# Seven products for eight in the second MLP product of a two-layer decoder trunk

## The chip, the core and the metric

One NeuronCore of a Trainium2 chip runs the whole program in one launch. The metric is the device time of one execution in microseconds (us), the median of several runs. Five engines work beside each other, each through its own queue in order: PE (TensorE, matmuls), DVE (VectorE), ACT (ScalarE), POOL (GpSimd) and SP (SyncE, which issues the loads).

## The reference, cut to what matters

The program is two layers of a decoder on 256 tokens of width 1024, in float32. Each layer has a mixer and an MLP; only the MLP is touched by the change.

```python
def sqrelu_mlp(hn, w1, w2):
    return jnp.square(jax.nn.relu(hn @ w1)) @ w2          # w1: 1024 x 4096, w2: 4096 x 1024

for i in range(DEPTH):                                    # DEPTH = 2
    ...                                                   # x = x + mixer(rms_norm(x))
    x = x + sqrelu_mlp(rms_norm(x, norm_mlp[i]), mlp_w1[i], mlp_w2[i])
return rms_norm(x, norm_final)
```

## The kernel before, in words

**Three matmuls for one product.** Every operand of a matmul is held as a rounded high part and a low part that is the rest, and a product is three matmuls into one PSUM bank: high by high, high by low, low by high (`mm3`, L532 to L536). So each weight block that is loaded must first be split: ACT copies it into the high part (L475), DVE subtracts that from the raw block and writes the low part (L478). Both of DVE's inputs lie in SBUF.

**Pieces.** All weights come as a stream of 128 x 1024 pieces in the order in which they are used (`_blocks`). `loads` (L452) brings each into one of five raw buffers by an SP transfer, as buffers come free; `splits` (L461) takes a pair of high and low buffers from the pool `parts`, issues the two split steps and gives the raw buffer back. A piece's pair goes back to `parts` when its last matmul is done. `parts` has six pairs, and two more while the MLP runs (`spare_m`).

**The MLP** (`mlp`, L1357). The 4096 hidden columns are worked in 16 pairs of 128-column tiles (`NI` = 16). For a pair i, the up-projection `cols_T` makes two 128 x 256 tiles in one bank: 2 columns of 8 steps of 3 matmuls of 256 columns, 48 in all. `square` (L1362) makes the squared relu: ACT takes the relu (L1368) and the square's high part (L1370), POOL multiplies the relu by itself in float32 (L1371), DVE subtracts (L1373). The down-projection (`down`, L1419) multiplies the pair by two pieces of the second weight: for a pair, 2 tiles (a) x 2 halves of the tokens (t) x 2 halves of the output columns (n), so 8 products of 3 matmuls of 512 columns, 24 in all, into four banks, one for each (t, n). The loop at L1427 interleaves the up-projection of pair i + 1 with the down-projection of pair i. The last three pairs (`TAIL` = 3) are kept for the end (the tail, L1444 to L1456), where one bank after the other is finished by 18 matmuls and added to x (L1310).

**The order of the work** is written by a planner when the kernel is built. Each step has a duration that the planner assumes (`t_act`, `t_dve`, a number for POOL), an urgency and events that it waits for; the planner runs these through a model and emits each engine's instructions in the order in which they came up. On the chip each engine keeps that order and waits by semaphores.

Of the kernel before, what the change touches and what calls it, by code (L numbers as in the profile page):

```python
# [73 lines left out]
def _blocks(ins):  # L74
# [6 lines left out]
    def n(w, k0, k1, cols):  # L81
        return np.asarray(w[k0 * 128:k1 * 128, cols]).reshape(k1 - k0, 128, -1).transpose(1, 0, 2)
# [7 lines left out]
    def span(a, b):  # L90
        return np.arange(a, b)
# [38 lines left out]
    mlp(0)  # L130
# [12 lines left out]
    return cut  # L143


def _lay_out(ins):
    f = {k: np.asarray(ins[k]) for k in ins}
    blocks = _blocks(ins)
# [167 lines left out]
class Slots:  # L316
# [4 lines left out]

    def get(self, n=1):
        ev = Event()
        self.waiting.append((ev, n))
        self.serve()
        return ev
# [23 lines left out]
    def serve(self):  # L350
        while self.waiting and len(self.items) >= self.waiting[0][1]:
            ev, n = self.waiting.pop(0)
            got, self.items = self.items[:n], self.items[n:]
            self.plan.fire(ev, "slot", got if n > 1 else got[0])
# [9 lines left out]
def trunk_kernel(ctx: ExitStack, tc: tile.TileContext, x, w, prm_d, gs, cst_d, eye, out, widths):  # L364
    nc = tc.nc

    hot = ctx.enter_context(tc.tile_pool(name="hot", bufs=1))
# [61 lines left out]
    class Piece:  # L429
        count, current, uses = 0, 0, 0  # L430

        def __init__(self):
            self.p, self.ready, self.slots = Piece.count, Event(), parts
            Piece.count += 1

        def use(self):
            Piece.current = max(Piece.current, self.p)
            Piece.uses += 1

        def release(self, ev):  # L440
# [11 lines left out]
    def loads():  # L452
        for p, n in enumerate(widths):
# [5 lines left out]
            plan.when([ev], None, lambda p=p, raw=got.value: plan.fire(loaded[p], SP, raw))  # L459

    def splits():  # L461
        for p, n in enumerate(widths):
            pc = pieces[p]
            yield loaded[p]
            got = pc.slots.get()
            yield got
# [414 lines left out]
    KK = [G1[:, 2560:3072].rearrange("p (a t) -> p a t", a=2), acts.tile([128, 2, S], F32R, name="KK")]  # L881
    KL = acts.tile([128, 2, 2, S], F32R, name="KL")
    KZ = acts.tile([128, 2, 2, S], F32R, name="KZ")
    gates = acts.tile([128, 2, 3, 2, 4], F32, name="gates")
# [16 lines left out]
    def first_norms():  # L901
        def keep_on():

            z = tbuf.items[1][0]
            yield zero_e
            while Piece.uses < KEEP:
                yield pe(0.23, lambda: nc.tensor.matmul(banks[1].t, z[:, :128], z, start=True, stop=True), u=9)  # L907

# [447 lines left out]

    def mlp(src, x_ready, nxt):  # L1357

        NI = FF // 256
        hs = [Event() for _ in range(NI)]  # L1360

        def square(i, b, deps, slots):  # L1362
            got = pbuf.get(2)
            tgot = tbuf.get()
            yield [got, tgot]
            r, sq = got.value
            hh, hl = tgot.value
            e = act(t_act(512), lambda: nc.scalar.activation(r, b.t, AF.Relu), got, *deps)  # L1368
            slots.put(b, [e])
            f = act(t_act(512, False), lambda: nc.scalar.activation(hh, r, AF.Square), e, tgot)  # L1370
            g = pool(1.225, lambda: nc.gpsimd.tensor_tensor(sq, r, r, OP.mult), e)  # L1371
            pbuf.put(r, [f, g])
            h = dve(t_dve(512), lambda: nc.vector.tensor_tensor(hl, sq, hh.bitcast(F32), OP.subtract), f, g)  # L1373
            pbuf.put(sq, [h])
            yield [f, h]
            plan.fire(hs[i], DVE, tgot.value)

        first = []

        def turned(t, b, evs):  # L1380
# [7 lines left out]
            if not t:  # L1388
                g = bank_s.get(2)
                first.append(g)  # L1390
                yield g
            bs = first[0].value
# [18 lines left out]
        tbuf.put(spare_t, [])  # L1411
        go, gs_ = bank_o.get(2), bank_s.get(2)
        slots = [bank_o, bank_s]
        acc, prev = None, [[go, go], [gs_, gs_]]

        def hid(i):
            return lambda: [a.rearrange("p (a t) -> p a t", a=2) for a in hs[i].value]

        def down(i, a, t, pc, ns=(0, 1)):  # L1419
            for n in ns:  # L1420
                prev[t][n] = row_mm(acc[t][n], hid(i), [hs[i]], pc, a, t, n, prev[t][n], i + a == 0, i == NI - 1 and a == 1)

        def give(i):
            evs = prev[0] + prev[1]
            plan.when([hs[i]], None, lambda: tbuf.put(hs[i].value, evs))

        for i in range(NI):  # L1427
            if i >= 1 and i + 1 < NI:
# [3 lines left out]
                plan.spawn(square(i + 1, got.value, evs, bank_a))  # L1432
            if acc is None:
                yield [go, gs_]
                acc = [go.value, gs_.value]
            if i >= NI - TAIL:
                continue
            for a in range(2):
                pc = next_piece()
                for t in range(2):  # L1440
                    down(i, a, t, pc)
                pc.release(plan.all([prev[1][0], prev[1][1]]))
            give(i)
        pcs = [next_piece() for _ in range(2 * TAIL)]  # L1444
        for t in range(2):
            evs = []
            for n in range(2):
                for i in range(NI - TAIL, NI):
                    for a in range(2):
                        down(i, a, t, pcs[2 * (i - NI + TAIL) + a], [n])  # L1450
                        if t and n:
                            pcs[2 * (i - NI + TAIL) + a].release(plan.all(prev[1]))
                    if t and n:
                        give(i)
                evs.append(add_to_x(acc[t][n], slots[t], prev[t][n], t, n, rs2[t]))
            nxt(t, evs)  # L1456
# [22 lines left out]
    def program():  # L1479
# [15 lines left out]
        f2, box2 = next_stage(2, True)  # L1495
        yield from mlp(box["src"], box["ready"], f2)
        reads.clear()


        MVH, MVL = (g.rearrange("p (t j c) -> p t j c", t=2, j=8) for g in (G0, G1))  # L1500
        t_free = tbuf.recall(spare_t)
        mz = [pool(0.9, lambda z=z: nc.gpsimd.memset(z.bitcast(F32)[:, :, :, 64:128], 0.0), t_free, u=2) for z in (MVH, MVL)]
        mv_e = []
# [3 lines left out]
        def got_mv(n):  # L1507
            def f(t, b, evs, slots):
# [82 lines left out]
```

## Time and profile before

| what | value |
|---|---|
| median of 3 runs | 633.95 us (633.5 to 634.44) |
| the profiled execution's own time | 634.41 us |
| its span, first to last instruction | 632.6 us |
| PE busy | 620.1 us, 98% of the span |
| DVE busy | 404.5 us, 64% |
| ACT busy | 361.7 us, 57% |
| POOL busy | 80.4 us, 13% |
| mean granted clock of PE | 0.997 of full speed |

Busy time of an engine is the time in which at least one of its instructions ran. A pipelined matmul's record is longer than the distance to the next one, so what a matmul costs is read from the starts. The loop of the MLP runs from about 162 to 311 us for the first layer and from about 460 to 609 us for the second.

### The profile page before, as it was taken

How to read it: one execution, taken by the hardware profiler on the slowest of the kernel's cores; microseconds unless marked ns; L12 is line 12 of the kernel's file. 1: busy time of each engine (PE TensorE's matmuls, PEld its weight loads, DVE VectorE, ACT ScalarE, POOL GpSimd, SP SyncE). 2: the span in 40 equal slices, each digit the busy share in tenths (PEclk: the TensorE clock that was granted, in tenths of full speed). 3: DMA queues.
4: the chain of work that ended last, by engine and by line, in shares of the span. 5: the costliest groups of instructions: out<-in, count | busy, mean ns of one | idle time of the engine just before them, and what ended most of it. 6: DMA issues, size and time to landing. Idle time of an engine off the chain costs nothing.

```text
span 632.6 us, 10575 instructions
## 1 busy us (share of the span) xinstructions
PE 620.1 (98%) x4046; PEld 562.6 (89%) x4046; DVE 404.5 (64%) x722; ACT 361.7 (57%) x649; POOL 80.4 (13%) x109
## 2 busy tenths in 40 slices
PE   9999999999999999999999999999999999999995
PEld 7999989887899898998988999988889899898994
DVE  5898899868554544545467588885964454554434
ACT  5779587656644545444444488773864544445421
POOL 2031031210200101011120012010020101001111
PEclk9999999999999999999999999999999999999998
DMA  8864633426665576565626443350786556565501
GB/s 324 283 244 133 202 101 110 176 92 204 222 204 196 168 204 192 191 186 205 189 82 212 168 137 131 130 189 17 229 271 214 185 189 188 181 209 167 166 1 67
DMA packets 32274, 110.03 MB, mean 174 GB/s; under 512 B 3408, under 2 KB 5728, under 8 KB 32224
## 3 DMA queue, kind: packets, MB, share of 16 engines
q1 hardware_dynamic: 31360, 106.74, 51.7%
q0 software_dynamic: 576, 2.10, 1.0%
q8 instruction: 31, 0.51, 0.3%
q10 hardware_dynamic: 288, 0.52, 0.2%
q14 instruction: 19, 0.16, 0.1%
HBM read 108.28 MB, written 1.07 MB: 173 GB/s over the span
## 4 chain that ended last, share of the span: by engine, by line
PE 86%; DVE 7%; ACT 4%; issue 2%; POOL 1%; POOLq 0%; DVEq 0%; ACTq 0%
PE ps L535 27%; PE ps L536 27%; PE ps L534 26%; DVE wlo L478 2%; PE ps L763 2%; PE ps L797 1%; ACT P L777 1%; PE ps L597 1%; PE ps L907 1%; PE ps L502 1%; ACT whi L475 1%; DVE P L773 1%; DVE G L974 0%; DVE Tl L525 0%; DVE x L1308 0%
## 5 line engine op out<-in xcount | busy, mean ns | idle before, releaser
L478 DVE TENSOR_TENSOR wlo<-raw,whi 128x1024 fp32r<-128x1024 f32 (+1 forms) x157 | 190.3, 1220 | 71.8 <-ACT whi L475 71.3
L475 ACT ACTIVATE whi<-raw 128x1024 fp32r<-128x1024 f32 (+1 forms) x157 | 163.3, 1051 | 93.2 <-PE ps L536 62.3
L534 PE MATMUL ps<-xTh,whi 128*128 128x256 f32 x592 | 169.1, 286 | 0.0
L536 PE MATMUL ps<-xTh,wlo 128*128 128x256 f32 x592 | 166.3, 281 | 0.0
L535 PE MATMUL ps<-xTl,whi 128*128 128x256 f32 x592 | 166.2, 281 | 0.0
L535 PEld LDWEIGHTS ps<-xTl,whi 128*128 128x128 f32 x592 | 111.7, 189 | 0.6
L534 PEld LDWEIGHTS ps<-xTh,whi 128*128 128x128 f32 x592 | 111.6, 188 | 0.6
L536 PEld LDWEIGHTS ps<-xTh,wlo 128*128 128x128 f32 x592 | 111.5, 188 | 0.0
L1371 POOL TENSOR_TENSOR P<-P 128x512 f32<-128x512 f32 x32 | 35.8, 1119 | 321.5 <-ACT P L1368 321.5
L478 DVE TENSOR_TENSOR mTl<-raw,mTh 128x1024 fp32r<-128x1024 f32 x34 | 42.5, 1249 | 22.9 <-ACT mTh L475 22.9
L475 ACT ACTIVATE mTh<-raw 128x1024 fp32r<-128x1024 f32 x34 | 36.1, 1062 | 29.7 <-PE ps L535 20.3
L1368 ACT ACTIVATE P<-ps 128x512 f32<-128x512 f32 x32 | 19.1, 598 | 52.3 <-PE ps L536 52.3
L1373 DVE TENSOR_TENSOR Tl<-P,Th 128x512 fp32r<-128x512 f32 x22 | 15.2, 692 | 50.2 <-POOL P L1371 50.2
L536 PE MATMUL ps<-whi,Tl 128*128 128x512 f32 x120 | 46.9, 390 | 0.0
L535 PE MATMUL ps<-wlo,Th 128*128 128x512 f32 x120 | 46.9, 390 | 0.0
L534 PE MATMUL ps<-whi,Th 128*128 128x512 f32 x120 | 46.8, 390 | 0.0
L777 ACT ACTIVATE P<-P,nm 128x128 f32<-128x128 f32 x80 | 35.4, 446 | 14.1 <-DVE nm L773 13.9
L535 PE MATMUL ps<-xTl,mTh 128*128 128x256 f32 (+1 forms) x128 | 37.9, 296 | 1.1 <-DVE xTl L478 1.1
L534 PE MATMUL ps<-xTh,mTh 128*128 128x256 f32 (+1 forms) x128 | 38.1, 297 | 0.0
L536 PE MATMUL ps<-xTh,mTl 128*128 128x256 f32 (+1 forms) x128 | 37.8, 295 | 0.0
L534 PE MATMUL ps<-whi,xTh 128*128 128x512 f32 (+1 forms) x88 | 34.3, 390 | 0.0
L535 PE MATMUL ps<-wlo,xTh 128*128 128x512 f32 (+1 forms) x88 | 33.1, 376 | 0.0
(221 smaller groups left out, 1196.7 us busy)
## 6 DMA issues: line engine op xcount, KB each, us to landing
raw<-in_w_dram SPq DMA_DIRECT2D x192, 512.0 KB, 4.1
gB<-in_gs_dram POOLq DMA_DIRECT2D x4, 512.0 KB, 4.0
x<-in_x_dram SPq DMA_DIRECT2D x2, 512.0 KB, 5.2
B<-ud SPq DMA_DIRECT2D x1, 1024.0 KB, 7.6
B<-ud SPq DMA_DIRECT2D x2, 512.0 KB, 9.1
raw<-in_w_dram SPq DMA_DIRECT2D x2, 420.0 KB, 7.0
gB<-in_gs_dram SPq DMA_DIRECT2D x1, 512.0 KB, 5.3
out_dram<-P SPq DMA_DIRECT2D x2, 256.0 KB, 2.1
```

The costliest lines, as they stand in the source:

```text
L475: nc.scalar.activation(pc.hi[:, :n], raw[:, :n], AF.Copy)
L478: nc.vector.tensor_tensor(pc.lo[:, :n], raw[:, :n], pc.hi[:, :n].bitcast(F32), OP.subtract)
L502: pe(0.43, lambda: nc.tensor.matmul(banks[7].t, tbuf.items[1][0][:, :128], tbuf.items[1][0], start=True, stop=True), zero_e)
L534: nc.tensor.matmul(out_, ah, bh, start=start, stop=False)
L535: nc.tensor.matmul(out_, ah, bl, start=False, stop=False)
L536: nc.tensor.matmul(out_, al, bh, start=False, stop=stop)
L597: nc.tensor.transpose(p[:, 128 * k:128 * k + 128], xs[:, 128 * k:128 * k + 128], ident)
L763: nc.tensor.matmul(ps[:, 128 * qt:128 * qt + nk], q[:, par, ts], k[i][:, par, :nk], start=i == 0, stop=i == 1)
L777: nc.scalar.activation(P[:, c], P[:, c], AF.Exp, bias=nm[:, qt:qt + 1], scale=-1.0, accum_out=sums[:, qt:qt + 1])
L1368: e = act(t_act(512), lambda: nc.scalar.activation(r, b.t, AF.Relu), got, *deps)
L1371: g = pool(1.225, lambda: nc.gpsimd.tensor_tensor(sq, r, r, OP.mult), e)
L1373: h = dve(t_dve(512), lambda: nc.vector.tensor_tensor(hl, sq, hh.bitcast(F32), OP.subtract), f, g)
```

## The change

For 13 of the 16 pairs (all but the tail), the down-projection's eight products are replaced by seven, after Strassen and Winograd. The pair's hidden values are a 2 x 2 grid of 128 x 128 blocks (half of the tokens by tile), the weight's pair of pieces a 2 x 2 grid of 128 x 512 blocks (tile by half of the columns). Four sums of hidden blocks and four sums of weight blocks give seven products, and each keeps a bank of its own through all 13 pairs, so that the sums of products are made once, after the last pair.

- PE: 21 matmuls of 512 columns for a pair in place of 24 (`fused`). Seven banks are taken by the products; one is left for the up-projections.
- Weight: `split_pair` splits four things in place of two: block b00 (512 wide), b10 with b11 (1024), then t1 with t3 and t4 with t2 (1024 each). The four sums are made in place in the two raw buffers by four POOL subtractions of 128 x 512 (L516 of the new kernel), each waiting for the one before.
- Hidden: `square` adds four DVE operations of 128 x 128 (L1484), a further ACT copy of 512 (L1487) and a further DVE subtraction of 512 (L1488) for each of the 13 pairs.
- End: four of the banks (b00, t1, t2, t3) are added to x in 11 DVE operations (L1584); the other three go on in the tail as the accumulators of three quarters of the output, and the fourth quarter gets a fresh bank.
- Buffers: four for the hidden values and a ninth pair for weights, in space that lies idle during the MLP. The up-projection now runs two pairs ahead. The pieces' order in the stream follows that.
- The planner's assumed time for the POOL multiplication goes from 1.225 to 1.4 us, the value it also has for the four subtractions, and one warm-up matmul's assumed time changes.

```diff
+    def split_pair(p):
+        ...
+        def place(k, names, src, deps):
+            hi, lo = k
+            n = 512 * len(names)
+            e = act(t_act(n, False), lambda: nc.scalar.activation(hi[:, :n], src, AF.Copy), *deps, u=u)
+            f = dve(t_dve(n), lambda: nc.vector.tensor_tensor(lo[:, :n], src, hi[:, :n].bitcast(F32), OP.subtract), e, u=u)
+            ...
+        def total(dst, a, b, *deps):
+            return pool(1.4, lambda: nc.gpsimd.tensor_tensor(dst, a, b, OP.subtract), *deps, u=u)
+        ...
+        f1 = place(k.value, ["b00"], r1[:, :512], [k, loaded[p]])
+        e1 = total(r1[:, :512], r1[:, 512:], r1[:, :512], f1)
+        ...
+        f2 = place(k.value, ["b10", "b11"], r2, [k, loaded[p + 1]])
+        e3 = total(r1[:, 512:], r2[:, 512:], r1[:, 512:], e1, loaded[p + 1])
+        e2 = total(r2[:, 512:], r2[:, 512:], r1[:, :512], e3, f2)
+        e4 = total(r2[:, :512], r2[:, :512], r2[:, 512:], e2)
+        ...
+        raws.put(r1, [place(k.value, ["t1", "t3"], r1, [k, e1, e3]), e2])
+        ...
+        raws.put(r2, [place(k.value, ["t4", "t2"], r2, [k, e4])])
...
-            g = pool(1.225, lambda: nc.gpsimd.tensor_tensor(sq, r, r, OP.mult), e)
+            g = pool(1.4, lambda: nc.gpsimd.tensor_tensor(sq, r, r, OP.mult), e, got)
...
+            for dst, x_, y_, op in ((s1, a10, a11, OP.add), (s2, s1, a00, OP.subtract), (s3, a00, a10, OP.subtract),
+                                    (s4, a01, s2, OP.subtract)):
+                e = dve(t_dve(128), lambda dst=dst, x_=x_, y_=y_, op=op: v(dst, x_, y_, op), e)
...
+            f2 = act(t_act(512, False), lambda: nc.scalar.activation(hh[:, 512:], ss, AF.Copy), e, hgot)
+            h2 = dve(t_dve(512), lambda: v(hl[:, 512:], ss, hh[:, 512:].bitcast(F32), OP.subtract), f2)
...
+        TERMS = (("b00", 0, (0, 1, 2, 3)), ("b10", 2, (0,)), ("t1", 4, (1, 3)), ("t3", 6, (2, 3)),
+                 ("t2", 5, (1, 2, 3)), ("b11", 7, (1,)), ("t4", 3, (2,)))
```

DVE in the first layer's loop, from the square of one pair (L1373) to that of the next; `wlo` and `mTl` are low parts of weights, `raw` the loaded pieces, `P` float32 work tiles, `G` and `Tl` the hidden values. Before:

```order
L1373 TENSOR_TENSOR G0_92<-P3_102,G0_92 128x512
L478 TENSOR_TENSOR wlo0_80<-raw0_94,whi0_74 128x1024
L478 TENSOR_TENSOR mTl_91<-raw1_95,mTh_90 128x1024
L478 TENSOR_TENSOR wlo1_81<-raw2_96,whi1_75 128x1024
L478 TENSOR_TENSOR mTl_91<-raw3_97,mTh_90 128x1024
```

and of the changed kernel (L1472 is the square's subtraction, L507 a split of the down-projection's weight, L559 one of the up-projection's):

```order
L1472 TENSOR_TENSOR G1_93<-P0_99,G1_93 128x512
L1484 TENSOR_TENSOR P1_100<-P0_99 128x128
L1484 TENSOR_TENSOR P1_100<-P1_100,P0_99 128x128
L1484 TENSOR_TENSOR P1_100<-P0_99 128x128
L1484 TENSOR_TENSOR P1_100<-P0_99,P1_100 128x128
L507 TENSOR_TENSOR wlo0_80<-raw0_94,whi0_74 128x512
L507 TENSOR_TENSOR G1_93<-raw2_96,KL_130 128x1024
L1488 TENSOR_TENSOR G1_93<-P1_100,G1_93 128x512
L559 TENSOR_TENSOR wlo2_82<-raw1_95,whi2_76 128x1024
L507 TENSOR_TENSOR wlo1_81<-raw0_94,whi1_75 128x1024
L559 TENSOR_TENSOR wlo3_83<-raw4_98,whi3_77 128x1024
L507 TENSOR_TENSOR mTl_91<-raw2_96,mTh_90 128x1024
```

Five operations for a pair became twelve: five of 1024, three of 512 and four of 128, and the last two splits of the down-projection's weight stand behind POOL's sums.

POOL in the same loop, five multiplications of five pairs before:

```order
L1371 TENSOR_TENSOR P0_99<-P2_101 128x512
L1371 TENSOR_TENSOR P4_103<-P1_100 128x512
L1371 TENSOR_TENSOR P2_101<-P3_102 128x512
L1371 TENSOR_TENSOR P1_100<-P0_99 128x512
L1371 TENSOR_TENSOR P3_102<-P4_103 128x512
```

and one pair of the changed kernel with the multiplication of the next pair behind it:

```order
L1470 TENSOR_TENSOR P3_102<-P1_100 128x512
L516 TENSOR_TENSOR raw1_95<-raw1_95 128x512
L516 TENSOR_TENSOR raw1_95<-raw3_97,raw1_95 128x512
L516 TENSOR_TENSOR raw3_97<-raw3_97,raw1_95 128x512
L516 TENSOR_TENSOR raw3_97<-raw3_97 128x512
L1470 TENSOR_TENSOR P0_99<-P2_101 128x512
```

One operation for a pair became five, all of 128 x 512.

DVE at the end of the first layer's MLP, where the tail's weight pieces are split and the banks are added to x (`x0` and `x1`, the two halves of the tokens). Before:

```order
L1373 TENSOR_TENSOR Tl0_88<-P4_103,Th0_86 128x512
L478 TENSOR_TENSOR wlo2_82<-raw3_97,whi2_76 128x1024
L478 TENSOR_TENSOR wlo3_83<-raw4_98,whi3_77 128x1024
L1373 TENSOR_TENSOR Tl1_89<-P2_101,Th1_87 128x512
L478 TENSOR_TENSOR wlo4_84<-raw0_94,whi4_78 128x1024
L1310 SCALAR_TENSOR_TENSOR x0_118<-ps2_112,rs2_1779,x0_118 128x512
```

and of the changed kernel, from the last split of a sum:

```order
L507 TENSOR_TENSOR mTl_91<-raw1_95,mTh_90 128x1024
L559 TENSOR_TENSOR G1_93<-raw0_94,KL_130 128x1024
L1584 SCALAR_TENSOR_TENSOR x0_118<-ps2_112,rs2_1776,x0_118 128x512 x2
L1472 TENSOR_TENSOR Tl1_89<-P0_99,Th1_87 128x512
L1584 SCALAR_TENSOR_TENSOR x1_119<-ps2_112,rs2_1780,x1_119 128x512 x2
L1584 SCALAR_TENSOR_TENSOR x0_118<-ps6_116,rs2_1776,x0_118 128x512
L1584 SCALAR_TENSOR_TENSOR x1_119<-ps6_116,rs2_1780,x1_119 128x512
L1584 SCALAR_TENSOR_TENSOR x1_119<-ps7_117,rs2_1780,x1_119 128x512 x2
L1584 SCALAR_TENSOR_TENSOR x0_118<-ps5_115,rs2_1776,x0_118 128x512
L1584 SCALAR_TENSOR_TENSOR x1_119<-ps5_115,rs2_1780,x1_119 128x512 x2
L559 TENSOR_TENSOR wlo1_81<-raw4_98,whi1_75 128x1024
L559 TENSOR_TENSOR mTl_91<-raw3_97,mTh_90 128x1024
```

Eleven additions to x now stand ahead of four of the tail's six splits; before, all of them stood ahead of the first addition.

## Rows read from the trace of the kernel before

**Rows 1.** The page: busy time of the engines (share, instructions).

```profile
PE 620.1 (98%) x4046; PEld 562.6 (89%) x4046; DVE 404.5 (64%) x722; ACT 361.7 (57%) x649; POOL 80.4 (13%) x109
```

**Rows 2.** Busy time by stretch: us, each engine, granted clock, DMA share, GB/s.

```profile
205.00:216.17 11.17, 11.17 (x74) 10.19 (x74) 5.50 (x5) 5.37 (x6) 1.04 (x1) 1.00 0.57 191
```

**Rows 3.** Timeline, PE: first matmuls of down- and up-projections (start, duration).

```profile
204.94 0.40 PE L534 MATMUL ps<-mTh,G 128*128 128x512 f32 x1
...
210.43 0.28 PE L534 MATMUL ps<-xTh,mTh 128*128 128x256 f32 x1
...
216.11 0.40 PE L534 MATMUL ps<-whi,Th 128*128 128x512 f32 x1
...
221.60 0.28 PE L534 MATMUL ps<-xTh,whi 128*128 128x256 f32 x1
```

**Rows 4.** Timeline, one steady pair: ACT, POOL and DVE, with the idle time before.

```profile
205.21 0.60 ACT L1368 ACTIVATE P<-ps 128x512 f32<-128x512 f32 x1 [1.96 <-PE ps L536]
205.84 0.63 ACT L1370 ACTIVATE Th<-P 128x512 fp32r<-128x512 f32 x1
206.37 1.04 ACT L475 ACTIVATE whi<-raw 128x1024 fp32r<-128x1024 f32 x1
...
205.95 1.04 POOL L1371 TENSOR_TENSOR P<-P 128x512 f32<-128x512 f32 x1 [10.12 <-ACT P L1368]
...
207.02 0.69 DVE L1373 TENSOR_TENSOR Tl<-P,Th 128x512 fp32r<-128x512 f32 x1 [2.52 <-POOL P L1371]
207.63 1.22 DVE L478 TENSOR_TENSOR wlo<-raw,whi 128x1024 fp32r<-128x1024 f32 x1
```

**Rows 5.** Timeline, DVE: two splits that follow each other at once.

```profile
137.34 2.35 DVE L478 TENSOR_TENSOR wlo<-raw,whi 128x1024 fp32r<-128x1024 f32 x2
```

**Rows 6.** The first layer's first squares: POOL, then DVE.

```profile
162.26 1.59 POOL L1371 TENSOR_TENSOR P<-P 128x512 f32<-128x512 f32 x1 [25.36 <-ACT P L1368]
164.94 1.68 POOL L1371 TENSOR_TENSOR P<-P 128x512 f32<-128x512 f32 x1 [1.08 <-ACT P L1368]
...
161.73 1.23 DVE L478 TENSOR_TENSOR wlo<-raw,whi 128x1024 fp32r<-128x1024 f32 x1 [0.72 <-ACT whi L475]
...
164.50 1.22 DVE L478 TENSOR_TENSOR mTl<-raw,mTh 128x1024 fp32r<-128x1024 f32 x1
```

**Rows 7.** The second layer's second square: POOL, then DVE.

```profile
463.33 1.04 POOL L1371 TENSOR_TENSOR P<-P 128x512 f32<-128x512 f32 x1 [1.74 <-ACT P L1368]
...
462.23 1.22 DVE L478 TENSOR_TENSOR wlo<-raw,whi 128x1024 fp32r<-128x1024 f32 x1
463.37 2.08 DVE L478 TENSOR_TENSOR mTl<-raw,mTh 128x1024 fp32r<-128x1024 f32 x1
```

**Rows 8.** POOL's operations on the work tiles P: ns min/median/max, first and last start.

```profile
L1371 POOL TENSOR_TENSOR P<-P x32: 1033/1042/1678, 162.3 to 609.9; 128x512 f32<-128x512 f32 x32
L834 POOL TENSOR_SCALAR P<-P,co x16: 369/502/1557, 368.7 to 428.2; 128x256 f32<-128x256 f32 x15, 128x128 f32<-128x128 f32 x1
```

**Rows 9.** Timeline in the second layer's mixer: POOL, then DVE.

```profile
380.90 1.55 POOL L834 TENSOR_SCALAR P<-P,co 128x256 f32<-128x256 f32 x1 [2.32 <-DVE co L827]
...
380.97 1.22 DVE L478 TENSOR_TENSOR wlo<-raw,whi 128x1024 fp32r<-128x1024 f32 x1
```

**Rows 10.** The first MLP's two ends: last norm step (DVE), first tail matmul (PE).

```profile
151.80 1.28 DVE L525 TENSOR_TENSOR xTl<-ps,xTh 128x512 fp32r<-128x512 f32 x2
...
311.12 0.40 PE L534 MATMUL ps<-whi,G 128*128 128x512 f32 x1
```

**Rows 11.** Additions to x in the tail: ns min/median/max, first and last start.

```profile
L1310 DVE SCALAR_TENSOR_TENSOR x<-ps,rs,x x8: 736/751/752, 316.1 to 625.4; 128x512 f32<-128x512 f32 x8
```

**Rows 12.** DMA issues: count, KB each, us to landing.

```profile
raw<-in_w_dram SPq DMA_DIRECT2D x192, 512.0 KB, 4.1
```

**Rows 13.** Busy time by stretch, as rows 2, where PE idled.

```profile
143.00:153.00 10.00, 8.84 (x47) 7.03 (x46) 9.86 (x19) 8.04 (x12) 0.00 (x0) 1.00 0.53 181
...
625.40:628.50 3.10, 0.00 (x0) 0.00 (x0) 2.46 (x5) 0.35 (x1) 0.95 (x1) 1.00 0.00 0
629.00:632.50 3.50, 0.00 (x0) 0.00 (x0) 0.00 (x0) 0.00 (x0) 0.00 (x0) 0.50 0.39 150
```

More of the change, by code (lines that the diff above doesn't have):

```diff
@@ L350, in serve @@
     def serve(self):
-        while self.waiting and len(self.items) >= self.waiting[0][1]:
-            ev, n = self.waiting.pop(0)
-            got, self.items = self.items[:n], self.items[n:]
+        while self.waiting:
+            ev, n, only = self.waiting[0]
+            got = [i for i in self.items if only is None or only(i)][:n]
+            if len(got) < n:
+                return
+            self.waiting.pop(0)
+            self.items = [i for i in self.items if not any(i is g for g in got)]
             self.plan.fire(ev, "slot", got if n > 1 else got[0])
@@ L438, in use, with block, got, done @@
             Piece.uses += 1
+        def block(self, name):
+            return self.blocks.setdefault(name, Event())
+        def got(self, names, f):
+            for nm in names:
+                ev = self.block(nm)
+                plan.when([f], None, lambda ev=ev: plan.fire(ev, DVE))
+        def done(self, name, ev):
+            k, names = self.left[name]
+            names.remove(name)
+            self.ends.setdefault(id(k), []).append(ev)
+            if not names:
+                parts.put(k, self.ends[id(k)])
         def release(self, ev):
@@ L463, in splits @@
             pc = pieces[p]
+            if kinds[p] == "pair":
+                yield from split_pair(p)
+            if kinds[p] in ("pair", "second"):
+                continue
             yield loaded[p]
-            got = pc.slots.get()
+            got = pc.slots.get(only=None if kinds[p] or pc.slots is not parts else usual)
             yield got
@@ L1355, in out_proj, with mlp @@
             parts.put(it, [done])
-    def mlp(src, x_ready, nxt):
+    def mlp(src, x_ready, nxt, free):
+        for it in spare_h:
+            hbuf.put(it, free)
+        parts.put(spare_w, free)
         NI = FF // 256
         hs = [Event() for _ in range(NI)]
+        ha = [Event() for _ in range(NI)]
+        turns = [Event() for _ in range(NI + 1)]
+        plan.fire(turns[0])
         def square(i, b, deps, slots):
[L1363 to L1367, printed above, removed]
+            fused = i < NI - TAIL
+            got = pbuf.get()
+            yield got
+            r = got.value
@@ L1431, in mlp @@
                 evs = [got] + [cols_T(src, got.value, next_piece(), col) for col in range(2)]
-                plan.spawn(square(i + 1, got.value, evs, bank_a))
+                plan.spawn(square(i + 2, got.value, evs, bank_a))
             if acc is None:
-                yield [go, gs_]
-                acc = [go.value, gs_.value]
-            if i >= NI - TAIL:
-                continue
[L1438 to L1442, printed above, removed]
@@ L1449, in mlp @@
                     for a in range(2):
-                        down(i, a, t, pcs[2 * (i - NI + TAIL) + a], [n])
+                        pc = pcs[2 * (i - NI + TAIL) + a]
+                        fresh = t and n and not a and i == NI - TAIL
+                        e = row_mm(b, hid(i), [hs[i]], pc, a, t, n, e, bool(fresh), i == NI - 1 and a == 1)
+                        ends.append(e)
                         if t and n:
-                            pcs[2 * (i - NI + TAIL) + a].release(plan.all(prev[1]))
+                            pc.release(e)
```

165 lines of the change are left out of this document (127 added, 38 removed).

## The prediction

> **What bounds the kernel now.** I read the page's busy times first: PE is busy for 98% of the span, DVE for 64% and POOL for 13% [rows 1]. An average over stages says little, so next the busy times of one steady pair of the first MLP, 205.00 to 216.17: PE 11.17 of 11.17 us, DVE 5.50, ACT 5.37, POOL 1.04, granted clock 1.00 [rows 2]. The loop is bound by PE alone, and the starts show what its matmuls cost: the 24 of the down-projection begin at 204.94 and the first of the up-projection at 210.43, so 5.49 us or 0.229 each; the 48 of the up-projection take from 210.43 to 216.11, 5.68 us [rows 3]. Then the order inside that pair: the relu's ACT step ends and POOL multiplies for 1.04 us, then DVE subtracts, and ahead of that subtraction DVE had stood idle for 2.52 us; a split of 1024 takes 1.04 on ACT and 1.22 on DVE [rows 4]. Averages, then, leave DVE and POOL much room. Whether they can use it together is the question, because the change hands both of them several times their work.
>
> **What is taken away.** 3 matmuls of 0.229 us for 26 pairs (13 in each layer): 78 x 0.229 = 17.8 us of PE. A pair would take PE 21 x 0.229 + 5.68 = 10.48 us in place of 11.17. As PE has no idle time in the loop, all of it would be gained if everything else stayed under 10.48 us for a pair.
>
> **ACT and the loads** stay under it. ACT: five splits of 1.04, the relu 0.60, and three steps of 512 at 0.63 (the square, the first weight block, the hidden sums): 7.7 us. The same four pieces are loaded for a pair, each landing in 4.1 us [rows 12]; with five raw buffers that is enough for a pair of 10 us or more, though the pair's own two buffers are now held until POOL's sums are split. I cost both at nothing; the cover is PE's or DVE's time.
>
> **DVE alone** stays under it too, though barely. Two splits in a row take 2.35 us, the second one 2.35 - 1.22 = 1.13 [rows 5]; an operation of 512 is followed by the next after 0.61 (207.02 to 207.63) [rows 4]. One of 128 is in no row: on the line through these two it takes 0.61 - 0.39 = 0.22, and 0.29 if the next one has to wait for its end (the line through the durations 1.22 and 0.69); I take 0.22. For a pair: 5 x 1.13 + 3 x 0.61 + 4 x 0.22 = 8.4 us.
>
> **DVE and POOL together don't.** POOL's multiplication takes 1.04 us in the median and up to 1.68 [rows 8]. The long ones show why. The one at 162.26 took 1.59 us; a DVE split had run since 161.73 and ended at 162.96; POOL ended 0.89 after that. The one at 164.94 took 1.68; DVE's split ended at 165.72, POOL 0.90 later [rows 6]. So POOL did nothing until 0.14 us before the split's end and then needed its usual 1.04. A POOL operation on other shapes took 1.55 us where the median is 0.50, and ended 0.26 after the split beside it [rows 8, 9]. The other way round it is the same: POOL began at 463.33, just as a split drained, and the next split, begun at 463.37, took 2.08 in place of 1.22 and ended 1.08 after POOL [rows 7]. A DVE operation with two inputs in SBUF and a POOL operation exclude each other, and each of the twelve DVE operations of the new pair is of that kind. A split and a POOL operation take turns in 0.90 + 1.08 = 1.98 us; two splits in a row take 1.13 each, so a POOL operation costs DVE 1.98 - 1.13 = 0.85 us. Before, there was one in a pair: 4 x 1.13 + 0.61 + 0.85 = 6.0 of 11.17 us, which PE hid. Now there are five: 8.4 + 5 x 0.85 = 12.6 us, against PE's 10.48 and the 11.17 of before. The matmuls saved are off the path; the turn-taking pair is the bound.
>
> The Trainium skill, page "SBUF — State Buffer", section "SBUF: two separate sides", says the same of the cause: GpSimd and VectorE share a port pair as an exclusive lock, which a VectorE operation with two SBUF inputs takes. It adds that the lock is held for the whole instruction. The rows differ there: the turns overlap by 0.14 us [rows 6]. What the whole instruction would give is the second rival.
>
> **The sum for one layer.** DVE is free for the pairs once the last norm step is done, at about 152 in the first layer (it starts two such steps at 151.80) [rows 10]. From there to the last split of pair 13 the changed order has 66 splits of 1024 (39 of the down-projection, 27 of the up-projection), 40 operations of 512, 52 of 128 and 66 of POOL: 66 x 1.13 + 40 x 0.61 + 52 x 0.22 + 66 x 0.85 = 74.6 + 24.4 + 11.4 + 56.1 = 166.5 us. With no idle moment that ends at 318.5. There will be some: POOL's four sums wait for each other, and the last split of a pair waits for the last sum and then for ACT's copy of 1.04, under which only the next pair's multiplication (0.90) fits. That is 0.2 us a pair, 12.8; 166.5 x 12.8 / 12.6 = 169 us, with 1 us for the first pair 322. If instead DVE went first at every contest, POOL's chain would run only where DVE has nothing left: 8.4 + three sums of 0.90 + two copies of 1.04 + five hand-overs of 0.14 = 13.9 us, and the end is 152 + 166.5 x 13.9 / 12.6 = 336. Ends 318.5 and 336; I take 322, as in rows 7 POOL got its turn between two splits that followed each other.
>
> After that PE has three products left (9 x 0.229 = 2.1), the last up-projection (5.7) and the tail, whose first matmul stands at 311.12 now [rows 10]. In the tail DVE has eleven additions ahead of four of the tail's splits: 11 x 0.75 [rows 11] + 1.13 + 0.61 = 10 us, then a split at 11.1; PE reaches that piece 2.1 + 5.7 + 6 x 0.229 = 9.2 us after the last sum's split. It waits 2 us there and about 1 for the next pieces and the last square: 3 us (0 to 3.3). The tail begins, in effect, at 322 + 7.8 + 3 = 332.8, so 21.7 us later than before. The second layer has the same counts, and PE is just as full behind either, so nothing gives this back: 2 x 21.7 = 43 us.
>
> The profiled execution took 634.4 us, 0.5 over the median of the runs (633.95), so it stands for them: 634.4 + 43 = **678 us**. With the low ends: 2 x (318.5 + 7.8 - 311.1) = 30, so 665. With the high ends: 2 x (336 + 7.8 + 3.3 - 311.1) = 72, so 706.
>
> **The rivals.** 1: PE stays the bound and the change gains. For it: each engine alone is under 10.48 us, and most of POOL's multiplications now run undisturbed at 1.04 [rows 8]. Against it: they do so because DVE is idle just then, waiting for them [rows 4]; wherever the two met, one waited [rows 6, 7, 9]. It gives 634.4 - 17.8 = 617, up to 623 with 3 us for each tail. The point that decides: 166.5 us would have to shrink to 148, which at the same DVE times means that a POOL operation costs DVE 0.57 us and not 0.85. Chance 0.07; 0.03 more for an end close to no change.
>
> 2: the turns don't overlap, and each instruction bars the other from its start to its end: 66 x 1.22 + 40 x 0.69 + 52 x 0.29 + 66 x 1.04 = 192 us, so 152 + 192 + 7.8 + 3 - 311.1 = 44 for a layer and 722 in all. Rows 6 and 7 speak against it with 0.14 us at each of three turns. Chance 0.03. This is the rule of the page "SBUF — State Buffer" named above, read by the letter.
>
> 3: DVE goes first whenever both want the port, 13.9 us for a pair: 700 to 706. Chance 0.15.
>
> 4: PE now idles some 2.3 us in each pair (12.8 - 10.5) and could lose its clock of 2.4 GHz. After the last matmul the granted clock was still 1.00 over 3.1 us without any, then 0.50 [rows 13]; gaps of 2.3 us are shorter. At half clock a pair would take PE 21 us, 8 more than 12.8. With one pair in eight so, 26 us more: 704. Chance 0.04. (The Trainium skill, page "TensorE: Matmul & The Clock Gate", section "Why this matters for your kernels", warns of idle gaps between bursts of matmuls; rows 13 bear on that only after the last one.)
>
> **How the numbers follow.** The forecast, turns at 12.6 to 13.3 us a pair, has a chance of 0.68: 665 to 690, most likely 678. With rivals 2 to 4 slower has 0.90, faster 0.07, the same 0.03 (0.2%, 1.3 us, is about what a measurement of this kernel can tell from no change). The range leaves out rival 1, rival 2 and no change; it reaches from 660, for a start some 2 us earlier in each layer, to 706.
>
> **What would show it.** In the trace of the changed kernel: POOL's operations of 128 x 512 at 1.04 where DVE rests, and 1.5 to 2 us otherwise; DVE's splits of 1024 at 1.22 or near 2.1; the two together leaving hardly a gap; PE in the loop busy for some 10.5 of 12.8 us, waiting for the low parts of t1 and t2; the distance between two relus in the steady loop 12.8 us. The matmuls of 512 still at 0.229. The step on which all rests is the exclusion: if POOL shows 1.04 beside a running split, and the pairs come at 10.5, I am wrong.

## The result, and the profile after

The changed kernel takes 705.26 us (median of 4 runs, 704.91 to 705.41) against 633.83 before: 1.1125 times as long, 95% interval 1.1106 to 1.1144. Its profiled span is 703.5 us, 70.9 more than before. The direction was forecast; the size was not: 71 us were lost where 43 were forecast, and the time lies just inside the upper edge of the range (706).

The page of the changed kernel, busy time of the engines and the chain that ended last:

```profile
PE 629.2 (89%) x3964; PEld 551.3 (78%) x3964; DVE 614.4 (87%) x926; ACT 408.5 (58%) x727; POOL 309.5 (44%) x213
...
POOL 32%; PE 32%; issue 18%; DVE 11%; ACT 5%; DMA 2%; POOLq 0%; SPq 0%; DVEq 0%; ACTq 0%
POOL raw L516 24%; PE ps L616 9%; PE ps L617 9%; PE ps L615 9%; POOL P L1470 8%; DVE wlo L559 3%; PE ps L844 1%; PE ps L878 1%; ACT P L858 1%; DVE wlo L507 1%; DVE P L1484 1%; DMA raw<-in_w_dram 1%; DVE G L1472 1%; DMA gB<-in_gs_dram 1%; PE ps L678 1%
```

Beside [rows 1], PE falls from 98% to 89% of a longer span with fewer matmuls, DVE rises from 404.5 to 614.4 us and POOL from 80.4 to 309.5. The average still hides the place; the steady loop of the first MLP shows it. The changed kernel by stretch (us, then busy time and instructions of PE, PEld, DVE, ACT, POOL, then granted clock, DMA share, GB/s):

```profile
240.00:320.00 80.00, 67.40 (x412) 56.73 (x411) 79.27 (x71) 42.22 (x54) 59.01 (x30) 0.99 0.48 155
```

Where PE had been busy for 11.17 of 11.17 us and DVE for 5.50 [rows 2], PE now idles for 12.6 of 80 us and DVE for 0.7. A pair's length is the distance between two relus. ACT's relus in that loop (start, duration):

```profile
262.77 0.57 ACT L1460 ACTIVATE P<-ps 128x512 f32<-128x512 f32 x1
...
276.44 0.57 ACT L1460 ACTIVATE P<-ps 128x512 f32<-128x512 f32 x1
...
290.09 0.58 ACT L1460 ACTIVATE P<-ps 128x512 f32<-128x512 f32 x1
...
303.74 0.58 ACT L1460 ACTIVATE P<-ps 128x512 f32<-128x512 f32 x1
```

13.65 us in place of 11.17. DVE's own work in them is 8.4 us by the prediction's sum; nearly all of the other 5.3 is waiting inside its instructions. The timeline of the changed kernel, POOL and then DVE, where they meet:

```profile
229.71 2.16 POOL L516 TENSOR_TENSOR raw<-raw 128x512 f32<-128x512 f32 x1
231.83 2.02 POOL L1470 TENSOR_TENSOR P<-P 128x512 f32<-128x512 f32 x1
238.28 2.20 POOL L516 TENSOR_TENSOR raw<-raw 128x512 f32<-128x512 f32 x1 [4.43 <-DVE mTl L507]
...
230.63 2.31 DVE L559 TENSOR_TENSOR G<-raw,KL 128x1024 fp32r<-128x1024 f32 x1
232.87 2.06 DVE L559 TENSOR_TENSOR wlo<-raw,whi 128x1024 fp32r<-128x1024 f32 x1
...
238.12 1.22 DVE L507 TENSOR_TENSOR wlo<-raw,whi 128x1024 fp32r<-128x1024 f32 x1
239.25 1.77 DVE L1488 TENSOR_TENSOR G<-P,G 128x512 fp32r<-128x512 f32 x1
```

Read them by their ends. POOL's sum ends at 231.87; DVE's split, begun at 230.63, ends at 232.94, 1.07 later. POOL's multiplication ends at 233.85, 0.91 after that split; DVE's next split at 234.93, 1.08 after the multiplication. These are the turns of [rows 6, 7], each to 0.02 us. What is new is the sum: begun at 238.28 beside a split that ends at 239.34, it ends at 240.48, 1.14 us after, where the multiplication needs 0.91. The group of the sums says the same. POOL's sums in the changed kernel (ns min/median/max, first and last start):

```profile
L516 POOL TENSOR_TENSOR raw<-raw x52: 1272/2157/2217, 153.0 to 661.3; 128x512 f32<-128x512 f32 x52
L516 POOL TENSOR_TENSOR raw<-raw,raw x52: 1259/1619/2172, 155.2 to 659.6; 128x512 f32<-128x512 f32 x52
```

Undisturbed, a sum takes 1.26 to 1.27 us; I had put it at the multiplication's 1.04 [rows 8]. A sum's turn then costs DVE 1.14 + 1.07 - 1.13 = 1.08 us and not 0.85, and a pair 8.4 + 0.85 + 4 x 1.08 = 13.6 us.

### The profile page after: what moved, and what is told of

Read it like the earlier page. It is cut to its first block, busy times and chain, and to the rows that moved or that the text cites. A ratio compares the mean times of both kernels' runs of the same rounds, so it can differ in the third digit from the quotient of the medians.

```text
span 703.5 us, 10842 instructions
## 1 busy us (share of the span) xinstructions
PE 629.2 (89%) x3964; PEld 551.3 (78%) x3964; DVE 614.4 (87%) x926; ACT 408.5 (58%) x727; POOL 309.5 (44%) x213
## 3 DMA queue, kind: packets, MB, share of 16 engines
HBM read 108.28 MB, written 1.07 MB: 155 GB/s over the span
## 4 chain that ended last, share of the span: by engine, by line
POOL 32%; PE 32%; issue 18%; DVE 11%; ACT 5%; DMA 2%; POOLq 0%; SPq 0%; DVEq 0%; ACTq 0%
POOL raw L516 24%; PE ps L616 9%; PE ps L617 9%; PE ps L615 9%; POOL P L1470 8%; DVE wlo L559 3%; PE ps L844 1%; PE ps L878 1%; ACT P L858 1%; DVE wlo L507 1%; DVE P L1484 1%; DMA raw<-in_w_dram 1%; DVE G L1472 1%; DMA gB<-in_gs_dram 1%; PE ps L678 1%
## 5 line engine op out<-in xcount | busy, mean ns | idle before, releaser
L559 DVE TENSOR_TENSOR wlo<-raw,whi 128x1024 fp32r<-128x1024 f32 (+2 forms) x122 | 188.9, 1564 | 5.8 <-ACT whi L556 5.5
L516 POOL TENSOR_TENSOR raw<-raw 128x512 f32<-128x512 f32 x52 | 110.4, 2123 | 128.2 <-DVE mTl L507 84.8
L556 ACT ACTIVATE whi<-raw 128x1024 fp32r<-128x1024 f32 (+2 forms) x122 | 125.1, 1045 | 24.7 <-DMA raw<-in_w_dram 13.3
L506 ACT ACTIVATE whi<-raw 128x1024 fp32r<-128x1024 f32 (+1 forms) x59 | 58.3, 995 | 72.0 <-POOL raw L516 69.4
L507 DVE TENSOR_TENSOR wlo<-raw,whi 128x1024 fp32r<-128x1024 f32 (+1 forms) x59 | 86.4, 1474 | 11.9 <-ACT whi L506 11.2
L516 POOL TENSOR_TENSOR raw<-raw,raw 128x512 f32<-128x512 f32 x52 | 89.6, 1723 | 9.6 <-DVE wlo L507 4.3
L616 PE MATMUL ps<-wlo,G 128*128 128x512 f32 x122 | 51.8, 424 | 21.5 <-DVE wlo L507 21.3
L617 PE MATMUL ps<-whi,G 128*128 128x512 f32 x122 | 50.1, 411 | 3.0 <-DVE G L1472 2.7
L615 PE MATMUL ps<-whi,G 128*128 128x512 f32 x122 | 49.3, 404 | 3.2 <-ACT whi L506 3.2
L1487 ACT ACTIVATE G<-P 128x512 fp32r<-128x512 f32 x26 | 16.4, 632 | 53.1 <-DVE P L1484 53.1
L507 DVE TENSOR_TENSOR mTl<-raw,mTh 128x512 fp32r<-128x512 f32 (+1 forms) x36 | 42.6, 1184 | 1.5 <-ACT mTh L506 1.2
L506 ACT ACTIVATE mTh<-raw 128x512 fp32r<-128x512 f32 (+1 forms) x36 | 29.8, 837 | 24.0 <-POOL raw L516 24.0
L858 ACT ACTIVATE P<-P,nm 128x128 f32<-128x128 f32 x80 | 35.4, 446 | 14.1 <-DVE nm L854 13.9
```

The lines of the kernel that those rows point to most:

```text
L506: e = act(t_act(n, False), lambda: nc.scalar.activation(hi[:, :n], src, AF.Copy), *deps, u=u)
L507: f = dve(t_dve(n), lambda: nc.vector.tensor_tensor(lo[:, :n], src, hi[:, :n].bitcast(F32), OP.subtract), e, u=u)
L516: return pool(1.4, lambda: nc.gpsimd.tensor_tensor(dst, a, b, OP.subtract), *deps, u=u)
L556: nc.scalar.activation(pc.hi[:, :n], raw[:, :n], AF.Copy)
L559: nc.vector.tensor_tensor(pc.lo[:, :n], raw[:, :n], pc.hi[:, :n].bitcast(F32), OP.subtract)
L615: nc.tensor.matmul(out_, ah, bh, start=start, stop=False)
```

## The experiments

My theory: DVE and POOL exclude each other, and each POOL operation of a pair takes from DVE about its own length. The rivals: POOL's sums are a chain in which each waits for the one before and ACT's and DVE's steps wait for them (a chain of waits of about 13.9 us, without any lock at its root); or the seven products cost something else.

| kernel | us | ratio to before (95%) | a steady pair, us |
|---|---|---|---|
| before | 633.8 to 634.8 | | 11.17 |
| after | 705.26 | 1.1125 (1.1106 to 1.1144) | 13.65 |
| unwaited_sums | 698.42 | one run | 13.64 |
| same_block | 678.41 | one run | 12.63 |
| sums_on_dve | 659.43 | one run | 11.9 to 12.05 |
| before_pool8 | 777.9 | one run | 15.8 (mean of 5) |
| before_pool4 | 639.74 | 1.0089 (1.0074 to 1.0105) | 11.17 |
| no_sums | 617.1 | one run | 10.5 |
| no_pool | 632.0 | 0.9973 (0.9959 to 0.9988) | 11.2 |
| no_pool_late | 632.06 | 0.9960 (0.9945 to 0.9975) | 11.2 |
| no_pool_late2 | 631.07 | 0.9949 (0.9934 to 0.9964) | 11.2 |
| every_second | 625.07 | 0.9855 (0.9839 to 0.9872) | 10.8 (mean of two) |

**unwaited_sums: the sums stay, no split waits for them** (only the next load into a raw buffer still does).

```diff
-            return pool(1.4, lambda: nc.gpsimd.tensor_tensor(dst, a, b, OP.subtract), *deps, u=u)
+            return pool(1.4, lambda: nc.gpsimd.tensor_tensor(VBf.rearrange("p a d -> p (a d)"), a, b, OP.subtract), *deps, u=u)
...
-        raws.put(r1, [place(k.value, ["t1", "t3"], r1, [k, e1, e3]), e2])
+        raws.put(r1, [place(k.value, ["t1", "t3"], r1, [k, loaded[p]]), e1, e3, e2])
```

> The four POOL sums of a pair are still made, but into a scratch tile, and the splits of the sums read the raw weight blocks and wait for no sum, so the output is not the reference's. If POOL and DVE exclude each other at the port, nothing is gained: a pair still costs 8.4 us of DVE, 0.85 for the multiplication and 4 x 1.07 for the sums, 13.5 us, and the kernel takes 695 to 706 us. If it is the chain of waits (sum, sum, copy, split) that sets the pace, the chain is gone, PE is the bound at 10.5 us a pair and the kernel takes 617 to 630 us.

698.42 us, and the pair still takes 13.64. This kernel's relus on ACT, and its busy times by stretch (the columns as above):

```profile
253.42 0.58 ACT L1460 ACTIVATE P<-ps 128x512 f32<-128x512 f32 x1
...
267.06 0.58 ACT L1460 ACTIVATE P<-ps 128x512 f32<-128x512 f32 x1
```

```profile
200.00:300.00 100.00, 80.33 (x475) 71.52 (x475) 97.40 (x89) 53.85 (x69) 62.85 (x36) 0.91 0.45 152
```

DVE is still busy for 97.40 of 100 us. The chain of waits is not what sets the loop, though POOL's sums have the largest share of the page's chain (24%, line 516): with those waits gone, the turns alone give the same length. The 6.8 us that came back lie outside the steady pairs; where, was not traced.

**same_block: each sum reads one block twice** (subtracted from itself, so the sums are zero), with all waits as they were.

```diff
-            return pool(1.4, lambda: nc.gpsimd.tensor_tensor(dst, a, b, OP.subtract), *deps, u=u)
+            return pool(1.4, lambda: nc.gpsimd.tensor_tensor(dst, dst, dst, OP.subtract), *deps, u=u)
```

> Each POOL sum subtracts one block from itself in place in place of one block from another, so the output is not the reference's; count, size, waits and the place of the result are the same. In the changed kernel an undisturbed sum takes 1.26 us where the multiplication of a tile by itself takes 1.04. If reading two different blocks is what makes it longer, the sums fall to 1.04, a pair to 12.7 to 12.8 us, and the kernel to about 682 us (705 - 26 x 0.88). If it is the place of the result or the subtraction, the sums stay at 1.26 and the kernel at 705.

678.41 us, a pair of 12.63. POOL's sums in this kernel (the columns as above), then its timeline: two relus on ACT, POOL and DVE:

```profile
L516 POOL TENSOR_TENSOR raw<-raw x104: 1031/1901/2022, 152.9 to 635.1; 128x512 f32<-128x512 f32 x104
```

```profile
254.54 0.58 ACT L1460 ACTIVATE P<-ps 128x512 f32<-128x512 f32 x1
...
267.18 0.58 ACT L1460 ACTIVATE P<-ps 128x512 f32<-128x512 f32 x1
...
237.42 2.02 POOL L516 TENSOR_TENSOR raw<-raw 128x512 f32<-128x512 f32 x1
239.40 2.02 POOL L1470 TENSOR_TENSOR P<-P 128x512 f32<-128x512 f32 x1
...
238.46 2.06 DVE L559 TENSOR_TENSOR wlo<-raw,whi 128x1024 fp32r<-128x1024 f32 x1
240.57 1.93 DVE L507 TENSOR_TENSOR mTl<-raw,mTh 128x1024 fp32r<-128x1024 f32 x1
```

The same instruction with the same shape, count and place takes 1.03 us undisturbed when both of its inputs are one block, and 1.26 when they are two. The ends stand 0.90 (240.52 to 241.42) and 1.08 us (241.42 to 242.50) apart, the very 1.98 us of a turn that I had read from [rows 6, 7]. With the duration that I had assumed, the chip gives a pair of 12.63 (forecast 12.8) and the time that I had forecast, 678. Of the 26.9 us between this kernel and the changed one, 104 sums at 0.22 are 22.9 directly; the other 4 come with them and were not split up further.

**before_pool8 and before_pool4: POOL's operations alone**, in the kernel before, with nothing else of the change. Eight, then four multiplications of two different blocks were put behind the multiplication of each pair, into a tile that nobody reads any more.

```diff
             g = pool(1.225, lambda: nc.gpsimd.tensor_tensor(sq, r, r, OP.mult), e)
+            for _ in range(8):
+                pool(1.225, lambda: nc.gpsimd.tensor_tensor(VBf.rearrange("p a d -> p (a d)"), cst[:, :512], B[:, 0:2].rearrange("p a b -> p (a b)"), OP.mult), g, u=5)
```

> The kernel before, with eight more POOL operations of 128 x 512 behind each pair's multiplication, on constants and into a scratch tile, for which nothing waits. By the port: 5.1 us of DVE, 0.85 and 8 x 1.07 = 14.5 us a pair in place of 11.17, so about 634 + 26 to 30 x 3.3 = 715 to 735 us. If POOL works beside DVE: 8 x 1.26 + 1.04 = 11.1 us of POOL a pair, just under PE, and 634 to 640 us.

777.9 us: far over both expectations, so a miss, though on the lock's side. The timeline of this kernel, POOL and then DVE, shows why:

```profile
242.28 14.62 POOL L1373 TENSOR_TENSOR VBf<-cst,B 128x512 f32<-128x512 f32 x8
256.86 1.04 POOL L1371 TENSOR_TENSOR P<-P 128x512 f32<-128x512 f32 x1
...
244.01 9.00 DVE L478 TENSOR_TENSOR wlo<-raw,whi 128x1024 fp32r<-128x1024 f32 x4
257.93 1.74 DVE L1375 TENSOR_TENSOR G<-P,G 128x512 fp32r<-128x512 f32 x1 [4.92 <-POOL P L1371]
```

The added operations take 14.62 us for eight. The next pair's multiplication stands behind them in POOL's queue, and DVE idles 4.92 us for it: the experiment had added a queue as well as a lock. Four operations leave POOL time.

> The kernel before with 4 (not 8) added GpSimd multiplications of two tiles of 128x512 per pair, into a scratch tile that nobody reads. Theory (GpSimd's operations stop VectorE's of two SBUF inputs, each for about its own length): VectorE 5.1 + 0.85 + 4 x 1.07 = 10.2 us per pair, under TensorE's 11.17, so within 3 us of the kernel before, 633 to 637 us. Rival (the cost grows in proportion to the number of operations from the first one on, half of what 8 cost): about 705 us.

639.74 us. The kernel with four, by stretch (the columns as above), and its ACT rows of two relus with the loop's end:

```profile
200.00:300.00 100.00, 100.00 (x646) 91.15 (x646) 93.46 (x49) 47.87 (x55) 85.47 (x48) 1.00 0.60 203
```

```profile
294.50 0.60 ACT L1368 ACTIVATE P<-ps 128x512 f32<-128x512 f32 x1 [1.96 <-PE ps L536]
305.67 0.60 ACT L1368 ACTIVATE P<-ps 128x512 f32<-128x512 f32 x1 [1.96 <-PE ps L536]
```

The last of these relus in the kernel before:

```profile
305.70 0.60 ACT L1368 ACTIVATE P<-ps 128x512 f32<-128x512 f32 x1 [1.96 <-PE ps L536]
```

In the loop it costs nothing: DVE is busy for 93.46 of 100 us, PE for all of them, and the relu before the tail stands at 305.67, where the kernel before has it at 305.70. That is the point that decides, seen from the cheap side: 5.1 + 0.85 + 4 x 1.08 = 10.3 us of DVE hide under 11.17 of PE, and the change's 13.6 don't hide under 10.5. The whole is 2.7 us over my expected end all the same, so the time is a miss, and for the most part not by the loop: in each tail the last pair's multiplication again stood behind the added ones, and PE waited 2.10 and 0.96 us for DVE's low part of that square. That is 3.1 of the 5.0 us by which this span is longer; the rest was not traced.

**no_sums: the four weight sums are left out**, and the splits read the raw blocks.

```diff
-        e1 = total(r1[:, :512], r1[:, 512:], r1[:, :512], f1)
+        e1 = f1
```

> The changed kernel with the four sums of weight blocks left out: the splits read the raw blocks, so the output is not the reference's. It shows what the seven products would give if the sums were free. By the port: 8.4 us of DVE and 0.85 for the multiplication, 9.3 us a pair, under PE's 10.5; PE is the bound, its clock stays whole, and the kernel takes 634 - 17.8 = 616 us, up to 623 with 3 us for the tail in each layer. If the products themselves, their banks or the further hidden sums cost something that the port does not explain, it stays over 625.

617.1 us, and in this stretch PE has no idle moment:

```profile
200.00:300.00 100.00, 100.00 (x663) 91.89 (x662) 83.35 (x115) 69.28 (x84) 9.96 (x10) 1.00 0.61 206
```

This is the first rival's time to the digit (617): 78 x 0.229 us are there to be had, and the sums alone stand in the way.

**sums_on_dve, no_pool, no_pool_late, no_pool_late2: POOL is taken out,** each on top of the one before. First the sums go to DVE:

```diff
-            return pool(1.4, lambda: nc.gpsimd.tensor_tensor(dst, a, b, OP.subtract), *deps, u=u)
+            return dve(t_dve(512), lambda: nc.vector.tensor_tensor(dst, a, b, OP.subtract), *deps, u=u)
```

> The four sums of weight blocks on DVE in place of POOL; POOL keeps the multiplication. By the port: DVE 8.4 + 4 x 0.61 and 0.85 for the multiplication, 11.7 us a pair in place of 13.65, so 705 - 26 x 1.95 = 654 us, 648 to 660. If DVE and POOL worked beside each other, DVE would be the fuller one for it (8.4 + 2.4 = 10.8 against 8.4) and the kernel would gain nothing or lose.

659.43 us, a pair of 11.9 to 12.05, some 1.6 less than after. An operation of 512 on DVE costs it 0.61; the same on POOL had cost it 1.08. By these two costs it would be 4 x 0.47 = 1.9 less. Handing the sums over to the idle engine was dearer for DVE than doing them itself. Then the relu's square goes to ACT as well, and GpSimd is out of the loop:

```diff
-            g = pool(1.4, lambda: nc.gpsimd.tensor_tensor(sq, r, r, OP.mult), e, got)
+            g = act(t_act(512, False), lambda: nc.scalar.activation(sq, r, AF.Square), e, got)
```

> Sums of weight blocks on DVE, and the multiplication of the relu by itself as a square on ACT, so POOL does nothing in the loop. By the port: DVE alone, 8.4 + 4 x 0.61 = 10.8 us a pair by the sum and 11.2 as measured with the sums on DVE (12.05 less 0.85); ACT 8.3. PE's 10.5 and DVE nearly balance; 705 - 26 x 2.5 to 2.8 = 632 to 640 us, about the kernel before.

632.0 us. The pair falls by about 0.8 to 11.2, as one multiplication's turn of 0.85 has it. DVE is still the bound, since PE needs only 10.48 us for a pair; this kernel by stretch:

```profile
240.00:260.00 20.00, 19.84 (x130) 17.81 (x129) 19.72 (x31) 13.53 (x18) 0.00 (x0) 1.00 0.63 209
260.00:280.00 20.00, 19.36 (x120) 16.54 (x120) 19.79 (x30) 13.77 (x19) 0.00 (x0) 1.00 0.61 203
```

I then took the eleven additions in the tail for what was left:

```diff
-                outs[o] = dve(t_dve(512), add, prev[nm], rs2[t][1], outs.get(o), u=0)
+                outs[o] = dve(t_dve(512), add, prev[nm], rs2[t][1], outs.get(o), u=4)
```

> The same, and the eleven additions to x get a lower urgency in the planner, so that most of the tail's splits stand ahead of them on DVE. If the additions cost 3 us in each layer's tail, 4 to 6 us less than the run before, 628 to 635; if PE's wait there has another cause, no change.

632.06 us, no change: giving the additions a later place in the planner got nothing back. The last try puts the hidden sums into an order in which none waits for the one just ahead of it:

```diff
-            for dst, x_, y_, op in ((s1, a10, a11, OP.add), (s2, s1, a00, OP.subtract), (s3, a00, a10, OP.subtract),
+            for dst, x_, y_, op in ((s1, a10, a11, OP.add), (s3, a00, a10, OP.subtract), (s2, s1, a00, OP.subtract),
```

> The same again, with the four hidden sums in an order in which none waits for the one just ahead of it (first, third, second, fourth). The wait for the first sum's end costs 0.1 us a pair in the changed kernel (0.31 to the next start in place of 0.20), so 0 to 2.6 us less.

631.07 us; the pair still takes 11.2, and the interval overlaps that of the two before. This order got nothing back either. DVE's own work is 8.4 + 4 x 0.61 = 10.8 us by the sum, which is over PE's 10.48 in any order.

**every_second: seven products where DVE has time,** on top of no_pool_late2. Only 7 of the 13 pairs use them; the others make eight ordinary products into the same banks (bank t1 is added to two quarters of the output, so two of the eight, one for each tile, are made with a difference of hidden blocks to make up for that).

```diff
-                    fused.add(len(out) - 1)
+                    if (i - 2) % 2 == 0:
+                        fused.add(len(out) - 1)
...
-            if i < NI - TAIL:
+            if i < NI - TAIL and i % 2:
+                whole(i)
+            elif i < NI - TAIL:
```

> Like no_pool_late2 (sums on VectorE, squares off GpSimd), but only the 7 even pairs of 13 use the seven products; the odd pairs use eight ordinary products with one hidden difference of 256 columns. Theory (VectorE's time per pair is what decides): VectorE's work is about 11.2 us in a full pair and some 6 us in a light one, 8.7 us on the mean, so TensorE is the bound again; it saves 14 x 3 x 0.229 = 9.6 us of the kernel before: 624 to 628 us, and TensorE shows no long idle gaps in the loop. Rival (the buffers can't carry a light pair's slack over to a full one, so each full pair still lasts VectorE's 11.2 us): about 630 to 634 us.

625.07 us, as expected, 1.45% under the kernel before. By stretch:

```profile
200.00:300.00 100.00, 100.00 (x647) 91.16 (x646) 78.34 (x103) 63.86 (x84) 0.00 (x0) 1.00 0.61 200
```

PE is full again and DVE at 78%: the buffers do carry a light pair's slack over to the full one. It saves 42 matmuls, 9.6 us, and 9.0 of them arrive. The best version found keeps the idea and halves its dose.

## Why the prediction came out as it did

**What bounds the kernel, and the direction: right.** PE's 17.8 us are real (no_sums) and off the path. DVE and POOL together are the bound: 79.27 of 80 us, and the same pair length with the waits removed.

**The exclusion and its turns: right.** 0.90 and 1.08 us were read from a handful of meetings in the kernel before, and hold in the loop of after to 0.02 us and in same_block exactly. DVE alone was nearly right (8.4 us): 11.2 in no_pool, less the 4 x 0.61 of its sums, leaves 8.8.

**A POOL operation at 0.85 us: the step that failed.** The 0.85 came from the multiplication [rows 8], which reads one tile twice. The sums read two blocks and take 1.26 us, 0.22 more, and all of that lies in DVE's turn. 52 sums in each layer: 11.4 us. The trace of before had no POOL operation of that kind and size; I took the nearest row as the value and gave it no upper bound. Rows of one operation on one shape are not yet rows of one cost: its inputs are part of it.

**322 for the last split of pair 13.** The timeline of the changed kernel, DVE and then PE's last long wait in the loop:

```profile
332.28 1.21 DVE L507 TENSOR_TENSOR mTl<-raw,mTh 128x1024 fp32r<-128x1024 f32 x1
...
337.31 6.00 DVE L1584 SCALAR_TENSOR_TENSOR x<-ps,rs,x 128x512 f32<-128x512 f32 x9
...
331.28 0.80 PE L616 MATMUL ps<-wlo,G 128*128 128x512 f32 x1 [3.84 <-DVE wlo L507]
```

It ends at 333.5, 11.5 later than forecast: the 11.4 of the sums. That agreement is closer than its parts. Between 152.2 and 333.5 DVE idles for 10.3 us, 8.2 of them in three waits for ACT's copies; I had allowed 3.5. So the turns taken together must have cost less than 66 full ones; a POOL operation that runs while DVE waits anyway costs nothing.

**The tail: 3 us forecast, 2.4 measured.** From the tail's first matmul to the last addition it is 17.9 us before (311.12 to 329.04) and 20.3 after (342.72 to 363.05). The additions are at 0.66 each (nine in 6.00) where I had 0.75.

**The sum.** In the first layer the last addition comes 34.0 us later: 333.5 + 7.8 - 311.1 = 30.2 by the last split, 1.4 by the clock (below), 2.4 by the tail; forecast were 18.7, none and 3. In the second layer it is 36.8 (625.43 and 696.25 less those 34.0), 2.8 more. About that much lies ahead of its MLP: from the first layer's last addition to the second MLP's first relu it is 130.3 us before (329.04 to 459.33) and 133.3 after (363.05 to 496.39); why is open. 34.0 + 36.8 = 70.8, and the spans differ by 70.9.

**The rivals.** The first (617) gives the right time for a kernel without sums and is wrong for this one. The second, each instruction barring the other from start to end, falls: the turns overlap by 0.14 us as before. (The Trainium skill, page "SBUF — State Buffer", section "SBUF: two separate sides", has the lock held for the whole instruction; the ends above, 0.91 us after a split for an operation of 1.04, don't agree with that last part.) The third named 700 to 706, and 705 it is, by another mechanism: it had POOL run only where DVE has nothing left. Then a DVE that idles and POOL operations at their own length would be seen; seen are, in the steady loop, a DVE with hardly an idle moment and POOL getting its turn between two splits. With unwaited_sums its chain is gone and the pair's length isn't. A time that fits is no proof of the story that came with it. And as the range's upper end, 706, stood there for this rival, it is luck that it also covered the sums' longer turns. The fourth, the clock, came partly true. PE's timeline in the changed kernel where it had idled, and then stretches behind such gaps (the columns as above):

```profile
195.20 0.50 PE L616 MATMUL ps<-wlo,G 128*128 128x512 f32 x1 [2.06 <-DVE wlo L507]
...
236.12 0.50 PE L616 MATMUL ps<-wlo,G 128*128 128x512 f32 x1 [2.34 <-DVE wlo L507]
```

```profile
190.00:196.50 6.50, 4.44 (x19) 3.11 (x18) 6.50 (x5) 2.57 (x4) 5.79 (x4) 1.00 0.67 219
196.50:200.00 3.50, 3.50 (x16) 3.22 (x15) 3.46 (x7) 1.11 (x2) 1.48 (x1) 0.52 0.33 126
...
237.50:241.00 3.50, 3.42 (x14) 2.62 (x13) 3.50 (x5) 2.06 (x3) 2.64 (x2) 0.51 0.59 193
...
331.20:336.60 5.40, 5.32 (x13) 4.17 (x14) 5.40 (x6) 4.11 (x5) 2.03 (x2) 0.50 0.94 301
```

Behind an idle gap of 2.06 us the granted clock is 0.52, the level of 1.2 GHz, where it had been 1.00; again behind one of 2.34, and behind the 3.84 shown above. I had given gaps of 2.3 us a chance of only 0.04, since the clock had held through 3.1 us without matmuls once [rows 13]; one such row was too little for that. The Trainium skill, page "TensorE: Matmul & The Clock Gate", section "Why this matters for your kernels", warns of idle gaps between bursts of matmuls, though it names longer ones; here the clock was at 0.52 behind 2.06 us. In the loop it cost nothing that can be seen, since PE waits for DVE there anyway (in unwaited_sums the mean granted clock of the loop was 0.91, and the pair as long); at the loop's end it did: from the last split to the tail's first matmul 9.2 us (333.5 to 342.7) in place of 7.8.

## What to carry to other kernels

An engine that looks idle is not free if its operations take turns with those of one that is nearly full, as GpSimd's did here with VectorE's subtractions of two SBUF inputs: count, for each stage, the busy engine's own time plus a turn for every operation of its neighbour, and compare that with the bound. Four operations of two blocks and a multiplication in each pair hid beside 5.1 us of VectorE's own work; the same five beside 8.4 didn't. Before a step goes to GpSimd, compare its turn (1.08 us here) with what VectorE needs to do the step itself (0.61). And a trade of matmuls for elementwise work need not be all or nothing: at every second pair it paid.

## What the runs showed of the hardware

GpSimd's tensor_tensor on 128 x 512 in float32 takes 1.03 to 1.04 us when both inputs are one block and 1.26 to 1.27 when they are two: for the subtraction (1031 against 1259 ns) and for the multiplication too, as the added multiplications of the kernel with four show (ns min/median/max):

```profile
L1373 POOL TENSOR_TENSOR VBf<-cst,B x128: 1257/2152/2278, 163.3 to 620.8; 128x512 f32<-128x512 f32 x128
```

So it is the number of blocks read and not the operation; two blocks of the same raw tile count as two (the sums raw<-raw of the changed kernel, 1272 ns at least). Why, no run here shows. And the granted clock fell to half behind gaps of PE of 2.06 and 2.34 us, though it had stayed at 1.00 over 3.1 us without matmuls in the kernel before.
